# A hybrid decoder layer on one core: small products stacked into single reduced-precision passes, GLA q and k in two-product form, and the order of 512- and 256-column matmuls

## The chip, the cores and the metric

The kernel runs on one core of a Trainium2 chip. The metric is the time of one execution on the device, in microseconds (us), lower is better. Four compute engines work side by side, each with its own instruction queue: TensorE (PE, with its weight loads shown apart as PEld), VectorE (DVE), ScalarE (ACT) and GpSimd (POOL). SyncE (SP) issues most DMA transfers.

## The reference

One layer over 256 tokens of width 1024, in float32:

```
n    = RMSNorm(x)
proj = n @ W_in        # moba q,k,v (512 each) | gla q,k (512 each), v (1024) | gate-down (16)
                       # | out-gate (1024) | two branch gates (1024 each)
A = causal softmax attention over one block of 256, 8 heads of 64, RMS-normed q,k, bias by T5 bucket
log_a = log_sigmoid(gate_down @ gate_up + bias) / 16
G = gated linear attention, 4 heads (dk 128, dv 256), chunks of 64, decay exp(cumsum(log_a)),
    RMS-normed, times silu(out-gate)
x = x + (sigmoid(gA) * (A @ W_bA) + sigmoid(gG) * (G @ W_bG)) @ W_out
x = x + relu(RMSNorm(x) @ W_up)^2 @ W_down
```

## The kernel before

Every float32 operand of a large product is split into a high part (type fp32r, one pass on TensorE) and a low part, the difference. A product is then high x high + high x low + low x high. ScalarE makes the high part of a weight unit (line 94, `wH`), VectorE subtracts to get the low part (line 98, `wL`).

**Units.** The weights come in 68 units of 1 MB (`hu` counts them; `load(i)` is the DMA on SyncE, `split(i, a)` the split of half a unit). A unit is split two units ahead of its use, and load i + 4 is issued once unit i is split. The first product (MQ, units 0 and 1) takes its operands from eight transfers `xw` that hold a k-tile of x transposed and of the weights each (`first_split`, `first_block`); ahead of it TensorE runs `NWARM` warm-up matmuls.

**Order.** A loop runs over 13 column groups of 512 (`IN_ORDER`: MQ, MK, GQ, GK, MV, ...), two units each, two blocks a unit. After each block come, in program order: `flush()` (what earlier steps deferred, VectorE's subtractions above all), `split(hu + 2, ...)`, the evacuation of a finished accumulator, and the small steps that a hand-written table puts in this slot: `at(slot, step)` with slot = 2 * hu + t. Then come the branch products, W_out, and the feed-forward in eight chunks: four blocks of W_up (`block_t`), then W_down of the chunk before (`down`).

**Blocks.** `block` (lines 114 to 120) is 12 matmuls of 512 columns with tokens as the output rows. GQ and GK are made transposed, with channels as the output rows, by `block_w` (lines 131 to 138): three matmuls of 256 columns for each k, 24 a block, 192 in all. The feed-forward's `block_t` (lines 122 to 129) has high and low part of the activation side by side in one operand `a` of 512 columns, so one matmul of 512 gives high x high in the left half of the bank and high x low in the right, and one of 256 adds low x high; `ff_evac` adds the halves (lines 865, 866). There are 256 such pairs.

**Small steps that the change touches.** `make_bias` (line 274): a one-hot matrix of 33 rows times the bias table, in float32; its result goes through DRAM (`spread_bias`, `load_bias`) to the softmax. `g_diag`, `g_row` (line 478): the row of 1/rms of the tokens, `rrow`, by a float32 product with ones. `low_split`, `g_low` (lines 487, 488): the 16 gate columns, both parts stacked twice in 64 weight columns, times xH and xL. `g_decay` (lines 506, 507): for each of four heads a product of 64 rows and one of 32 rows. `g_evac` (line 544): GQ and GK times `rrow`, one VectorE operation for two heads. `g_scores` (lines 578 to 581): for each of 2 token tiles and 4 heads, three float32 products of 64 columns; a float32 matmul is two instructions. `m_transpose` (line 328) and `m_ptrans` (line 407) are float32 transposes by TensorE, four to a step.

Of the kernel before, what the change touches and what calls it, by code (L numbers as in the profile page):

```python
# [19 lines left out]
S = 256  # L20
D = 1024
NT = 2
# [7 lines left out]
NWARM = 7  # L30
# [16 lines left out]
def block_kernel(ctx, tc, xw0_d, xw_d, x_d, vec_d, wlow_d, w_d, up_d, t5_d, onehot_d, out_d):  # L47
# [6 lines left out]
    t4 = ctx.enter_context(tc.tile_pool(name="t4", bufs=22))  # L54
# [67 lines left out]
    def block_t(i, j, g, a, acc):  # L122


        for k in range(4):
# [5 lines left out]
    def block_w(i, j, g, aH, aL, acc):  # L131

        for k in range(4):
            h, c = divmod(4 * g + k, 2)
            c = slice(c * 256 + j * P, c * 256 + (j + 1) * P)
            nc.tensor.matmul(acc, wH[i][:, h, c], aH[:, k, :], start=g == 0 and k == 0, stop=False)  # L136
            nc.tensor.matmul(acc, wH[i][:, h, c], aL[:, k, :], start=False, stop=False)  # L137
            nc.tensor.matmul(acc, wL[i][:, h, c], aH[:, k, :], start=False, stop=g == 1 and k == 3)  # L138
# [5 lines left out]
    vec = const.tile([P, NVEC], F32, name="vec")  # L144
    nc.gpsimd.dma_start(vec, vec_d)
    XW = S + 512
# [11 lines left out]
    wlow = const.tile([P, 8, 16], F32, name="wlow")  # L158
    onehot = mid("onehot")[:NB + 1, :384]
    t5 = const.tile([NB + 1, H], F32, name="t5")  # L160
    nc.vector.memset(t5[NB:NB + 1, :], 1.0)
    gup = mid("gup")
    ones = const.tile([P, P], F32, name="ones")
    nc.vector.memset(ones, 1.0)
    touch = const.tile([P, 1], F32, name="touch")
    nc.scalar.activation(touch, ones[:, 0:1], AF.Exp)
# [21 lines left out]
    xH = [kview(big(f"xH{g}", F32R)) for g in range(2)]  # L188
    xL = [kview(big(f"xL{g}", F32R)) for g in range(2)]
# [61 lines left out]

    T = {}
    lowS = const.tile([P, 8, 64], F32R, name="lowS")

    def low_split():
        v = lowS.rearrange("p k (r a c) -> p k r a c", r=2, a=2)
        for r in range(2):
            nc.scalar.activation(v[:, :, r, 0, :], wlow, AF.Copy)
            nc.vector.tensor_tensor(v[:, :, r, 1, :], wlow, v[:, :, r, 0, :].bitcast(F32), op=OP.subtract)
        nc.vector.tensor_copy(causal, cf)  # L260

    def gup_split():
        both = big("gupHL", F32R)
        T["gupH"], T["gupL"] = gupH, gupL = both[:64, :512], both[:32, 512:]
        nc.scalar.activation(gupH, gup[:64, :], AF.Copy)
        nc.vector.tensor_tensor(gupL, gup[:32, :], gupH[:32, :].bitcast(F32), op=OP.subtract)
# [3 lines left out]
    bias = t4.tile([P, H, 256], F32, name="bias", tag="t8", bufs=2)  # L270
# [197 lines left out]
    def g_diag():  # L468
        T["diag"] = mid("diag")
        for t in range(NT):  # L470
            nc.vector.tensor_scalar(T["diag"][:, t * P:(t + 1) * P], ident, rstd[:, t:t + 1], None, op0=OP.mult)
# [3 lines left out]
    def g_row():  # L475

        pr = axbank("prow")
        nc.tensor.matmul(pr[:, :S], ones, T["diag"][:, :S], start=True, stop=True)
        nc.scalar.activation(rrow, pr[:, :S], AF.Copy)

    def g_low():

        p = axbank("plow")
        o = p[:64, :S]
# [4 lines left out]
        low = mid("low")[:64, :S]  # L489
        nc.vector.tensor_tensor(low, o, rrow[:64, :], op=OP.mult)  # L490

        both = t2.tile([P, 512], F32R, name="lowHL", tag="t2")
        T["lowT"], high = both[:64, :S], both[:64, S:]
        nc.scalar.activation(T["lowT"][:32], low[:32], AF.Copy)
        nc.scalar.activation(high[32:], low[32:], AF.Copy)
        nc.vector.tensor_tensor(T["lowT"][32:], low[32:], high[32:].bitcast(F32), op=OP.subtract)

    def g_decay(half):
# [3 lines left out]
        for j in range(2):  # L502
            h = 2 * half + j
            hs = slice(h * DK, (h + 1) * DK)
            o = p[:, j * S:(j + 1) * S]
            nc.tensor.matmul(o, T["gupH"][:, hs], T["lowT"], start=True, stop=False)
            nc.tensor.matmul(o, T["gupL"][:, hs], T["lowT"][:32], start=False, stop=True)
# [31 lines left out]
    def g_evac(which, half, acc):  # L539

        if half == 0:
            T[which] = big(which)
        v = T[which][:, half * 512:half * 512 + 512].rearrange("p (h t) -> p h t", h=2)
# [29 lines left out]

# [441 lines left out]
```

## Time and profile before

| | |
|---|---|
| median of 3 runs | 422.23 us (421.67 to 422.37) |
| profiled execution, its own time | 421.65 us |
| its span, first to last instruction | 419.8 us |
| busy: PE, DVE, ACT | 415.1, 281.8, 220.3 us |

The profile is of one execution. "Busy" of PE counts pipelined matmuls whose ends are modelled, so a matmul's price is better read from the start of one to the start of the next. A row of the timeline gives start, duration, engine, line, output and operands; in brackets the idle time before it and what ended it. The chain of waits is followed back from the last instruction, each piece with its start and length.

### The profile page before, as it was taken

How to read it: one execution, taken by the hardware profiler on the slowest of the kernel's cores; microseconds unless marked ns; L12 is line 12 of the kernel's file. 1: busy time of each engine (PE TensorE's matmuls, PEld its weight loads, DVE VectorE, ACT ScalarE, POOL GpSimd, SP SyncE). 2: the span in 40 equal slices, each digit the busy share in tenths (PEclk: the TensorE clock that was granted, in tenths of full speed). 3: DMA queues.
4: the chain of work that ended last, by engine and by line, in shares of the span. 5: the costliest groups of instructions: out<-in, count | busy, mean ns of one | idle time of the engine just before them, and what ended most of it. 6: DMA issues, size and time to landing. Idle time of an engine off the chain costs nothing.

```text
span 419.8 us, 5413 instructions
## 1 busy us (share of the span) xinstructions
PE 415.1 (99%) x2155; PEld 348.6 (83%) x2155; DVE 281.8 (67%) x360; ACT 220.3 (52%) x334; POOL 18.4 (4%) x22
## 2 busy tenths in 40 slices
PE   8999999999999999999999999999999999999996
PEld 5879988788888888888888888888888888888886
DVE  5739777889778653864676878757493838374753
ACT  6668456587854464552524456546453617263520
POOL 2008000000002001000000000000000000000000
PEclk9999999999999999999999999999999999999999
DMA  8895974454355343381755535736364553628002
GB/s 283 341 393 212 314 262 176 165 180 157 107 194 192 106 141 120 146 297 45 259 201 200 200 116 205 276 114 257 138 226 176 173 228 133 269 100 301 0 0 101
DMA packets 13860, 78.73 MB, mean 188 GB/s; under 512 B 1555, under 2 KB 3148, under 8 KB 5388
## 3 DMA queue, kind: packets, MB, share of 16 engines
q1 hardware_dynamic: 13372, 77.08, 50.3%
q10 hardware_dynamic: 432, 1.31, 0.9%
q8 instruction: 17, 0.28, 0.3%
q14 instruction: 7, 0.06, 0.0%
q0 software_dynamic: 32, 0.01, 0.0%
HBM read 77.33 MB, written 2.63 MB: 190 GB/s over the span
## 4 chain that ended last, share of the span: by engine, by line
PE 98%; DMA 1%; ACT 0%; DVE 0%; issue 0%
PE pu L128 14%; PE acc L118 9%; PE acc L120 9%; PE acc L119 9%; PE pu L129 7%; PE fa L118 7%; PE fa L120 7%; PE fa L119 7%; PE acc L136 2%; PE acc L137 2%; PE acc L138 2%; PE po L118 2%; PE po L120 2%; PE po L119 2%; PE pg L119 2%; PE pg L118 2%
## 5 line engine op out<-in xcount | busy, mean ns | idle before, releaser
L98 DVE TENSOR_TENSOR wl<-raw,wh 128x1024 fp32r<-128x1024 f32 x132 | 158.2, 1220 | 19.5 <-ACT wh L94 19.1
L94 ACT ACTIVATE wh<-raw 128x1024 fp32r<-128x1024 f32 x132 | 135.4, 1052 | 24.3 <-PE pg L120 9.8
L128 PE MATMUL pu<-hHL,wh 128*128 128x512 f32 x256 | 90.9, 399 | 0.0
L129 PE MATMUL pu<-hHL,wl 128*128 128x256 f32 x256 | 71.9, 281 | 0.0
L118 PE MATMUL acc<-wh,xH 128*128 128x512 f32 x160 | 64.1, 401 | 0.0
L119 PE MATMUL acc<-wl,xH 128*128 128x512 f32 x160 | 62.4, 390 | 0.0
L120 PE MATMUL acc<-wh,xL 128*128 128x512 f32 x160 | 62.4, 390 | 0.0
L128 PEld LDWEIGHTS pu<-hHL,wh 128*128 128x128 f32 x256 | 48.1, 188 | 11.8
L129 PEld LDWEIGHTS pu<-hHL,wl 128*128 128x128 f32 x256 | 48.3, 189 | 0.3
L118 PE MATMUL fa<-wh,fH 128*128 128x512 f32 x124 | 48.5, 391 | 0.0
L120 PE MATMUL fa<-wh,fL 128*128 128x512 f32 x124 | 48.4, 390 | 0.0
L119 PE MATMUL fa<-wl,fH 128*128 128x512 f32 x124 | 48.3, 389 | 0.0
L865 ACT ACTIVATE half<-pu 128x256 f32<-128x256 f32 x32 | 12.0, 378 | 55.3 <-PE pu L129 55.3
L866 DVE TENSOR_TENSOR sq<-pu,half 128x256 f32<-128x256 f32 x32 | 13.4, 422 | 35.7 <-ACT half L865 35.5
L120 PEld LDWEIGHTS acc<-wh,xL 128*128 128x128 f32 x160 | 30.0, 188 | 6.6
L118 PEld LDWEIGHTS acc<-wh,xH 128*128 128x128 f32 x160 | 30.1, 188 | 6.0
L119 PEld LDWEIGHTS acc<-wl,xH 128*128 128x128 f32 x160 | 30.1, 188 | 5.5
L120 PEld LDWEIGHTS fa<-wh,fL 128*128 128x128 f32 x124 | 23.3, 188 | 5.1
L118 PEld LDWEIGHTS fa<-wh,fH 128*128 128x128 f32 x124 | 23.3, 188 | 4.9
L119 PEld LDWEIGHTS fa<-wl,fH 128*128 128x128 f32 x124 | 23.3, 188 | 4.7
L871 ACT ACTIVATE fH<-sq 128x512 fp32r<-128x512 f32 x16 | 10.1, 634 | 20.3 <-DVE sq L868 20.3
L136 PE MATMUL acc<-xH,wh 128*128 128x256 f32 x64 | 18.6, 291 | 0.0
(234 smaller groups left out, 572.4 us busy)
## 6 DMA issues: line engine op xcount, KB each, us to landing
raw<-w SPq DMA_DIRECT2D x65, 1024.0 KB, 4.9
xw<-xw SPq DMA_DIRECT2D x7, 384.0 KB, 6.5
ur<-ud SPq DMA_DIRECT2D x1, 1536.0 KB, 10.7
raw<-w SPq DMA_DIRECT2D x2, 512.0 KB, 6.3
xs<-xs SPq DMA_DIRECT2D x2, 512.0 KB, 8.6
bias<-ur SPq DMA_DIRECT2D x1, 1024.0 KB, 7.5
xr<-xs ACTq DMA_DIRECT2D x2, 512.0 KB, 4.6
out<-o SPq DMA_DIRECT2D x3, 256.0 KB, 2.1
```

Source lines behind the costliest of these rows:

```text
L94: nc.scalar.activation(wH[i][:, s, :], raw[i][:, s, :], AF.Copy)
L98: nc.vector.tensor_tensor(wL[i][:, s, :], raw[i][:, s, :], wH[i][:, s, :].bitcast(F32), op=OP.subtract)
L118: nc.tensor.matmul(acc, aH[:, k, tk], h, start=start and k == 0, stop=False)
L119: nc.tensor.matmul(acc, aH[:, k, tk], low, start=False, stop=False)
L120: nc.tensor.matmul(acc, aL[:, k, tk], h, start=False, stop=stop and k == 3)
L128: nc.tensor.matmul(acc, wH[i][:, h, c], a[:, k, :], start=g == 0 and k == 0, stop=False)
L129: nc.tensor.matmul(acc[:, S:], wL[i][:, h, c], a[:, k, :S], start=False, stop=g == 1 and k == 3)
L136: nc.tensor.matmul(acc, wH[i][:, h, c], aH[:, k, :], start=g == 0 and k == 0, stop=False)
L137: nc.tensor.matmul(acc, wH[i][:, h, c], aL[:, k, :], start=False, stop=False)
L865: nc.scalar.activation(half, acc[:, S:], AF.Copy)
L866: nc.vector.tensor_tensor(o, acc[:, :S], half, op=OP.add)
L871: nc.scalar.activation(H, v, AF.Copy)
```

## The change

- `NWARM` goes from 7 to 9.
- Eight small transfers become three. The 16 gate columns (`wlow`) come with the constants `vec` on GpSimd's queue; bias table and one-hot matrix come in one transfer of 97 rows (two copies, 31 rows of zeros between them), the gate-up matrix in one of 96 rows (six copies). Both are split into high and low part for one fp32r product each: `make_bias` (97 rows, 384 columns), `g_decay` (96 rows, 256 columns, one matmul a head).
- `g_row` uses fp32r, with the diagonal split in two.
- GQ and GK use `block_t`; xH and xL stand side by side in one tile. Their evacuation, `g_evac`, now adds the halves of each head.
- `block_t` issues its four 512s first, then its four 256s, which add to the left half.
- `g_scores` has one float32 product of 128 columns a head, and one of 64 columns and 64 rows that overwrites a corner of it, after all four.
- Small steps move to other slots: `make_bias` 7 to 8, `g_decay(0)` 13 to 12, four of the transposes one slot later. `t4` has 20 buffers instead of 22, `t8` three instead of two.

```diff
-NWARM = 7
+NWARM = 9
@@ block_t
         for k in range(4):
-            h, c = divmod(4 * g + k, 2)
-            c = slice(c * 256 + j * P, c * 256 + (j + 1) * P)
-            nc.tensor.matmul(acc, wH[i][:, h, c], a[:, k, :], start=g == 0 and k == 0, stop=False)
-            nc.tensor.matmul(acc[:, S:], wL[i][:, h, c], a[:, k, :S], start=False, stop=g == 1 and k == 3)
+            nc.tensor.matmul(acc, tile_(wH, k), a[:, k, :], start=g == 0 and k == 0, stop=False)
         for k in range(4):
+            nc.tensor.matmul(acc[:, :S], tile_(wL, k), a[:, k, :S], start=False, stop=g == 1 and k == 3)
@@ transfers
-    nc.sync.dma_start(onehot, onehot_d)
-    nc.sync.dma_start(t5[:NB, :], t5_d)
-    nc.sync.dma_start(wlow, wlow_d)
-    for r in range(4):
-        nc.sync.dma_start(gup[16 * r:16 * r + 16, :], up_d)
+    nc.sync.dma_start(biasR, bias_d)
+    nc.sync.dma_start(gup, up_d)
     load(4)
     load(5)
@@ splits of the small operands
+        for r in range(3):
             nc.scalar.activation(v[:, :, r, 0, :], wlow, AF.Copy)
             nc.vector.tensor_tensor(v[:, :, r, 1, :], wlow, v[:, :, r, 0, :].bitcast(F32), op=OP.subtract)
...
+        nc.scalar.activation(gupS, gup, AF.Copy)
+        nc.vector.tensor_tensor(gupS[64:], gup[64:], gupS[64:].bitcast(F32), op=OP.subtract)
+    def split_bias():
+        nc.scalar.activation(biasS, biasR, AF.Copy)
+        nc.vector.tensor_tensor(biasS[64:, :H], biasR[64:, :H], biasS[64:, :H].bitcast(F32), op=OP.subtract)
@@ make_bias
-        nc.tensor.matmul(pb[:H, :384], t5, onehot, start=True, stop=True)
+        nc.tensor.matmul(pb[:H, :384], biasS[:, :H], biasS[:, H:], start=True, stop=True)
@@ g_diag, g_row
+        nc.scalar.activation(d[:, :S], full, AF.Copy)
+        nc.vector.tensor_tensor(d[:, S:], full, d[:, :S].bitcast(F32), op=OP.subtract)
...
-        nc.tensor.matmul(pr[:, :S], ones, T["diag"][:, :S], start=True, stop=True)
+        for a in range(2):
+            nc.tensor.matmul(pr[:, :S], ones, T["diag"][:, a * S:(a + 1) * S], start=a == 0, stop=a == 1)
@@ g_low
-        nc.scalar.activation(T["lowT"][:32], low[:32], AF.Copy)
-        nc.scalar.activation(high[32:], low[32:], AF.Copy)
-        nc.vector.tensor_tensor(T["lowT"][32:], low[32:], high[32:].bitcast(F32), op=OP.subtract)
+        nc.scalar.activation(both, low, AF.Copy)
+        nc.vector.tensor_tensor(both[32:64], low[32:64], both[32:64].bitcast(F32), op=OP.subtract)
@@ g_decay
-            nc.tensor.matmul(o, T["gupH"][:, hs], T["lowT"], start=True, stop=False)
-            nc.tensor.matmul(o, T["gupL"][:, hs], T["lowT"][:32], start=False, stop=True)
+            nc.tensor.matmul(p[:, j * S:(j + 1) * S], gupS[:, h * DK:(h + 1) * DK], T["low"],
+                             start=True, stop=True)
@@ g_evac
-        nc.vector.scalar_tensor_tensor(v, acc.rearrange("p (h t) -> p h t", h=2),
-                                       DK ** -0.5 if which == "gq" else 1.0,
-                                       rrow[:, None, :].to_broadcast([P, 2, S]), op0=OP.mult, op1=OP.mult)
+        half = mid("half")[:, :S]
+        nc.scalar.activation(half, acc[:, S:], AF.Copy)
+
+        def finish():
+            nc.vector.tensor_tensor(v, acc[:, :S], half, op=OP.add)
+            nc.vector.scalar_tensor_tensor(v, v, DK ** -0.5 if which == "gq" else 1.0, rrow,
+                                           op0=OP.mult, op1=OP.mult)
+
+        defer(finish)
@@ g_scores
-            nc.tensor.matmul(p[:, o:o + CH], ki[:, b:b + P], q[:, b:b + CH], start=True, stop=True)
+            nc.tensor.matmul(p[:, o:o + P], ki[:, b:b + P], q[:, b:b + P], start=True, stop=True)
+        for h in range(GH):
+            b, o = h * S + t * P, h * P
             nc.tensor.matmul(p[:CH, o + CH:o + P], kd[:, b:b + CH], q[:, b + CH:b + P],
                              start=True, stop=True)
-            nc.tensor.matmul(p[CH:, o + CH:o + P], ki[:, b + CH:b + P], q[:, b + CH:b + P],
-                             start=True, stop=True)
@@ slots
-    at(7, make_bias)
+    at(5, split_bias)
+    at(8, make_bias)
...
-    at(12, m_transpose, "mq", 0)
     at(12, m_norm, "mk", 1)
+    at(12, g_decay, 0)
+    at(13, m_transpose, "mq", 0)
     at(13, m_transpose, "mq", 1)
-    at(13, g_decay, 0)
     at(14, g_decay, 1)
-    at(14, m_transpose, "mk", 0)
     at(14, load_bias)
+    at(15, m_transpose, "mk", 0)
     at(15, m_transpose, "mk", 1)
...
-    at(28, m_ptrans, 0)
     at(29, g_exp, "edec")
+    at(29, m_ptrans, 0)
     at(29, m_ptrans, 1)
-    at(30, m_ptrans, 2)
+    at(31, m_ptrans, 2)
     at(31, m_ptrans, 3)
     at(31, g_qk, "eb")
-    at(32, m_ptrans, 4)
+    at(33, m_ptrans, 4)
     at(33, m_ptrans, 5)
@@ main loop, GQ and GK
                 if col in TRANSPOSED:
+                    acc = mmbank("acct")
                     for k in range(2):
-                        block_w(hu, t, k, xH[k], xL[k], acc[g][:, t * S:(t + 1) * S])
+                        block_t(hu, t, k, xHL[k], acc)
...
                 elif col in TRANSPOSED:
-                    if t == 1:
-                        evac[col](g, acc[g])
+                    evac[col](2 * g + t, acc)
```

## Rows read from the trace of the kernel before

**Rows 1.** The page's chain of waits, share of the span by engine.

```profile
PE 98%; DMA 1%; ACT 0%; DVE 0%; issue 0%
```

**Rows 2.** Timeline of TensorE, from the start to the second product.

```profile
0.85 3.15 PE L172 MATMUL pwarm<-const-bfloat16-1.0 128*128 128x512 bf16 x7 [0.85 <-PEq L1007]
...
4.64 0.80 PE L213 MATMUL acc<-wh,xH 128*128 128x512 f32 x1 [0.64 <-ACT wh L202]
...
8.21 0.40 PE L213 MATMUL acc<-wh,xH 128*128 128x512 f32 x1
...
17.34 0.39 PE L118 MATMUL acc<-wh,xH 128*128 128x512 f32 x1
```

**Rows 3.** Chain of waits in order of time: start, length, what.

```profile
28.38 0.74 PE pbias L274 x2
29.12 0.32 PE acc L136
...
32.19 0.43 PE prow L478 x2
...
45.95 0.44 PE pt L328 x4
...
49.69 0.31 PE pz L506
...
50.93 0.32 PE acc L136
...
55.23 0.59 PE pt L328 x4
```

**Rows 4.** Chain of waits, in the feed-forward.

```profile
272.86 0.24 PE pu L128
...
276.04 0.24 PE pu L128
```

**Rows 5.** Timeline of TensorE, a run of 256s and the 512s behind it.

```profile
149.61 0.28 PE L616 MATMUL po<-gvH,atH 128*128 128x256 f32 x1
...
150.08 0.28 PE L616 MATMUL po<-gvL,atH 128*128 128x256 f32 x1
...
151.04 0.40 PE L118 MATMUL acc<-wh,xH 128*128 128x512 f32 x1
...
151.97 0.39 PE L119 MATMUL acc<-wl,xH 128*128 128x512 f32 x1
```

**Rows 6.** Windows: length, busy PE, PEld, DVE, ACT, POOL; clock, DMA share, GB/s.

```profile
24.90:29.13 4.23, 4.23 (x19) 2.73 (x17) 1.40 (x3) 4.09 (x6) 0.70 (x1) 1.00 1.00 420
29.13:44.36 15.23, 15.23 (x127) 15.18 (x128) 14.96 (x26) 11.58 (x18) 9.15 (x5) 1.00 0.67 247
```

**Rows 7.** Timeline of VectorE, the low-rank product.

```profile
44.36 0.41 DVE L490 TENSOR_TENSOR low<-plow,rrow 64x256 f32<-64x256 f32 x1
...
45.74 0.41 DVE L496 TENSOR_TENSOR lowHL<-low,lowHL 32x256 fp32r<-32x256 f32 x1 [0.97 <-ACT lowHL L495]
```

**Rows 8.** Chain of waits, GLA scores of the first token tile.

```profile
132.89 0.17 PE pa L578 x2
133.06 0.20 PE pa L579
...
135.22 0.43 PE acc L118
```

**Rows 9.** Waits of SyncE's queue: total, times, longest (us).

```profile
SPq L85 <- DMA xs<-xs: 1.4, 1, 1.4
```

**Rows 10.** The page's DMA issues: count, KB each, median us to landing.

```profile
raw<-w SPq DMA_DIRECT2D x65, 1024.0 KB, 4.9
```

**Rows 11.** Timeline of ScalarE, the first split of load 4.

```profile
25.00 1.06 ACT L94 ACTIVATE wh<-raw 128x1024 fp32r<-128x1024 f32 x1 [5.77 <-DMA raw<-w]
```

**Rows 12.** Groups of VectorE by shape: busy us, mean ns, idle before.

```profile
L866 DVE TENSOR_TENSOR sq<-pu,half 128x256 f32<-128x256 f32 x32 | 13.4, 422 | 35.7 <-ACT half L865 35.5
...
L544 DVE SCALAR_TENSOR_TENSOR gq<-acc,rrow 128x512 f32<-128x512 f32 x2 | 1.4, 678 | 0.0
```

More of the change, by code (lines that the diff above doesn't have):

```diff
@@ L157, in block_kernel @@
     load(3)
[L158 to L164, printed above, removed]
+    NBR = 64 + NB + 1
+    smallR, smallS = big("smallR"), big("smallS", F32R)
+    biasR, biasS = smallR[:NBR, :H + 384], smallS[:NBR, :H + 384]
+    gup, gupS = smallR[:96, 512:], smallS[:96, 512:]
+    ones = const.tile([P, P], F32R, name="ones")
+    nc.vector.memset(ones.bitcast(F32), 1.0)
     touch = const.tile([P, 1], F32, name="touch")
-    nc.scalar.activation(touch, ones[:, 0:1], AF.Exp)
+    nc.scalar.activation(touch, ones[:, 0:1].bitcast(F32), AF.Exp)
     pw = axbank("pwarm")
@@ L185, in block_kernel @@
     nc.gpsimd.memset(seg.rearrange("p (c s) -> p c s", s=CH)[:, :, 0:1], 0.0)
-    xH = [kview(big(f"xH{g}", F32R)) for g in range(2)]
-    xL = [kview(big(f"xL{g}", F32R)) for g in range(2)]
+    xHL = [t4.tile([P, 4, 2 * S], F32R, name=f"xHL{g}", tag="t8", bufs=3) for g in range(2)]
+    xH, xL = [v[:, :, :S] for v in xHL], [v[:, :, S:] for v in xHL]
     for i in range(2):
@@ L252, in block_kernel @@
     T = {}
-    lowS = const.tile([P, 8, 64], F32R, name="lowS")
+    lowS = const.tile([P, 8, 96], F32R, name="lowS")
     def low_split():
-        v = lowS.rearrange("p k (r a c) -> p k r a c", r=2, a=2)
-        for r in range(2):
+        v = lowS.rearrange("p k (r a c) -> p k r a c", r=3, a=2)
+        for r in range(3):
             nc.scalar.activation(v[:, :, r, 0, :], wlow, AF.Copy)
@@ L468, in g_diag @@
     def g_diag():
-        T["diag"] = mid("diag")
+        T["diag"] = d = t2.tile([P, 512], F32R, name="diag", tag="t2")
+        full = mid("diagf")[:, :S]
         for t in range(NT):
-            nc.vector.tensor_scalar(T["diag"][:, t * P:(t + 1) * P], ident, rstd[:, t:t + 1], None, op0=OP.mult)
+            nc.vector.tensor_scalar(full[:, t * P:(t + 1) * P], ident, rstd[:, t:t + 1], None, op0=OP.mult)
+        nc.scalar.activation(d[:, :S], full, AF.Copy)
+        nc.vector.tensor_tensor(d[:, S:], full, d[:, :S].bitcast(F32), op=OP.subtract)
     rrow = const.tile([P, S], F32, name="rrow")
@@ L744, in block_kernel @@
     for u, col in enumerate(IN_ORDER):
-        acc = [(axbank if u == 1 else mmbank)(f"acc{t}") for t in range(NT)]
+        acc = [] if col in TRANSPOSED else [(axbank if u == 1 else mmbank)(f"acc{t}") for t in range(NT)]
         for g in range(2):
@@ L809, in block_kernel @@
     hres = [big(f"h{t}") for t in range(NT)]
-    hHL = [t4.tile([P, 4, 2 * S], F32R, name=f"hHL{g}", tag="t8", bufs=2) for g in range(2)]
+    hHL = [t4.tile([P, 4, 2 * S], F32R, name=f"hHL{g}", tag="t8", bufs=3) for g in range(2)]
     hss = [small(f"hss{t}", 2) for t in range(NT)]
@@ L992 @@
     cols = lambda v, n: A(v)[0].reshape(n, 128).T
+    bias = np.concatenate([np.concatenate([A(t5_bias), np.ones((1, 8), np.float32)]), _onehot()], axis=1)
     arrays = {
@@ L998 @@
             cols(norm2_g, 8), cols(gla_gate_bias, 4), cols(gla_out_norm_g, 2),
[L999 to L1000 removed]
+            np.tile(A(moba_q_norm_g)[0], 2)[:, None], np.tile(A(moba_k_norm_g)[0], 2)[:, None],
+            w[:, GLOW:GLOW + 16].reshape(8, 128, 16).transpose(1, 0, 2).reshape(128, 128)], axis=1),
         "w": np.stack(units),
[L1002 to L1004 removed]
+        "gup": np.tile(A(gla_gate_up)[0], (6, 1)),
+        "bias": np.concatenate([bias, np.zeros((31, 8 + 384), np.float32), bias]),
     }
```

44 lines of the change are left out of this document (15 added, 29 removed).

## The prediction, made before the change was built or run

> **What bounds the kernel now.** I read the chain of waits first: 98% of it is TensorE [rows 1], so time goes down only where TensorE's own work shrinks, and only as long as no other engine becomes what TensorE waits for. Then I read the stretches that the change touches. At the start, seven warm-ups run from 0.85 us, TensorE then idles for 0.64 us, the first product starts at 4.64 us at about 0.43 us a matmul (1.2 GHz) and falls to 0.23 us (2.4 GHz) at 8.21 us [rows 2]; from there 40 matmuls of 512 columns take 9.13 us, 0.228 us each. Around the GLA columns, the chain in order of time shows small products as pieces that are dear for their size [rows 3]. In the feed-forward, 512s and 256s alternate: 9 pairs in 3.18 us, 0.353 us a pair [rows 4]; elsewhere twelve 256s stand in a row, and 512s follow them [rows 5]. The reader should see next that VectorE is full just there: busy for 14.96 of the 15.23 us before it evacuates the low-rank product [rows 6]. TensorE doesn't wait for it today, because the product that needs the result stands some 3.4 us behind it (the split ends at 45.74 + 0.41 = 46.15 us [rows 7], the product starts at 49.69 us in the chain [rows 3]). The change moves that product one block earlier.
>
> **The change part by part.**
>
> *Bias product.* Two passes of float32 take 0.74 us, and the next matmul takes 0.32 us in place of 0.12 us: 0.94 us [rows 3]. One pass of 384 columns over 97 rows takes by columns about 0.17 us (384/512 of 0.228 us [rows 2]). Saved: 0.77 us; 0.57 us if the 0.2 us of the change of shape stays.
>
> *Row of rstd.* 0.43 us [rows 3] becomes two 256s at 0.12 us [rows 5]: 0.19 us saved.
>
> *Decay product.* Today each half is four matmuls at 0.31 us, and the matmul behind it is 0.20 us (first half) or 0.15 us (second) late: 1.44 + 1.39 = 2.83 us [rows 3]. After it each half is two matmuls of 256 columns and 96 rows. No row has 96. The bounds are 0.12 us (128 rows [rows 5]) and 0.31 us (64 and 32 rows in turn). In the latter each matmul differs in shape from the one before, which the four new ones don't, so I take 0.12: 0.48 us, 2.35 us saved; with 0.31 us and the 0.35 us of late followers 1.24 us. The Trainium skill, "TensorEngine Tiling (Array Packing)", section Tiling Modes, knows row tiles of 128, 64 and 32 and a drain between modes, so 96 rows would count as 128; no row shows it, and by it the sum is the one taken.
>
> *GLA q and k.* 192 matmuls at 0.12 us are 23.04 us. After it there are 16 groups of four 512s and four 256s. Four 512s right behind 256s took 0.93 us (151.04 to 151.97), four 256s behind a 512 took 0.47 us (149.61 to 150.08) [rows 5]: 1.40 us a group, 22.45 us, 0.6 us saved. Bounds: with no price for the alternation 4 x 0.228 + 4 x 0.12 = 1.39 us (0.8 saved), with the alternating price 1.41 us (0.4 saved).
>
> *Feed-forward order.* 64 such groups: 1.413 us now (four pairs of 0.353 us), 1.40 us after, some 11 ns each, 0.7 us; 0 to 1.6 us by the same bounds. One rule speaks against it. The Trainium skill, "TensorE: Matmul & The Clock Gate", section LDWEIGHTS, prices a weight load by its columns, 128 in 107 ns, as much as 256 columns stream in; by it the order would be neutral and the sum 0.7 us smaller. The rows give 0.12 us to a 256 in a run and 0.353 us to a pair, so the measured difference stays in.
>
> *Scores.* In the chain, from 132.89 to the next block at 135.22 us, plus 0.20 us by which that block's first matmul is long (0.43 us against 0.23): 2.53 us, twice [rows 8]. The first one with 64 weight columns takes 0.20 us in the chain [rows 8] where half of the 0.11 us of a float32 instruction of 128 columns (0.44 us for four transposes [rows 3]) would be its share, so a change of shape costs some 0.15 us, four times each way. After: eight at 0.11, one change in, eight of the small ones at most 0.11 each, one change out with the 0.20: 0.88 + 0.15 + 0.88 + 0.20 = 2.11 us. Saved 0.4 us each, 0.8 us; with small ones at half and no changes 1.32 us, 2.4 us saved; at the other end 0.
>
> *Warm-ups.* Two more at 0.43 us fill the 0.64 us idle and end about when the first operands do; delay up to 0.2 us. If the clock rises by 4.64 us instead of at 8.21 us, at most half of these 3.57 us comes back, 1.8 us; at least nothing. I cost it at nothing, since the wait below swallows it.
>
> *Transfers.* SyncE issues load 4 (the first GLA weights) only when an x transfer has landed [rows 9], behind seven small transfers, so the queue is empty before it. Such loads take 4.9 us from issue to landing [rows 10], 2.5 us of it data at 420 GB/s [rows 6]; some 2.4 us are start-up that a load in a busy queue doesn't show. After the change two small transfers remain and load 4 can queue up behind x. Against that, the small ones carry some 100 KB more (about 340 KB instead of 243 KB by their shapes), and the gate weights' 64 KB go ahead with the constants on GpSimd's queue, 0.4 us together at 420 GB/s. ScalarE starts on load 4 at 25.00 us today, after 5.77 us of waiting [rows 11]; I take 1.8 us earlier, 23.2 us, of at most 2.4 us and at least none.
>
> *VectorE's queue, and what is late next.* The stretch of 15.23 us starts 4.1 us behind ScalarE's first split of load 4 (29.13 against 25.00 us), so 1.8 us earlier; ScalarE's new split of the bias operands (392 elements, about 0.45 us) stands ahead of it: 27.8 us. Into the stretch come the diagonal's split (a wait for ScalarE and a subtraction, 0.85 us), a third copy of the gate weights (0.2 us), and the GLA evacuation: three heads at two operations of about 0.4 us net of overlap (0.42 us for 256 elements) in place of two at 0.6 us (0.68 us) [rows 12], 1.0 us. So the low product is evacuated at 27.8 + 15.23 + 2.05 = 45.1 us. From there to the split operand it is 1.79 us today (44.36 to 46.15 us [rows 7]), less one of two ScalarE copies: ready at 46.45 us. TensorE gets to the decay product, now behind the block that ends at 45.95 us [rows 3], at 45.95 - 0.77 - 0.19 - 0.37 (ten of the 16 groups) = 44.6 us. So it waits for 46.45 - 44.6 = **1.9 us of new idle time**. Behind this wait stand all GK blocks but the first, so the whole rest of the kernel moves with it.
>
> *At nothing:* the moved transposes (0.44 us for four wherever they stand [rows 3]); their splits are used a block or two later, and if that cover goes a split costs 0.6 us of VectorE. The bias product one block later: its round trip through DRAM waits for its turn on SyncE's queue anyway; if not, the softmax starts late, blocks ahead of its use. The low product keeps its 16 matmuls of 256 columns. Buffer counts: four long-lived tiles leave the pool that loses two.
>
> **Sum.** Up to the GLA v columns: -(0.77 + 0.19 + 2.35 + 0.6) + 1.9 = -2.0 us. Scores -0.8, feed-forward -0.7: **-3.5 us**. Against the profiled execution's own 421.65 us (span 419.8 us, 1.85 us around it) that is 418.15 us; the median lies 0.58 us higher, so I predict **418.7 us**. What a measurement of this kernel can tell from no change is about 0.2%, 0.84 us.
>
> **Rivals.**
> 1. *No new wait* (0.13). VectorE gets through sooner, and all that TensorE saves counts, with up to 1.1 us of the clock's: -5.4 to -6.5 us, some 416.3 us. For: load 4 might land even earlier. Against: VectorE's 98% in that stretch.
> 2. *Load 4 is no earlier* (0.10): the new wait is 3.7 us, the sum -1.7 us, 420.5 us. For: small rows still stand ahead. Against: the wait on x that goes away.
> 3. *The small prices don't fall* (0.12): 96 rows cost 0.31 us (-1.1 of the gain) and the feed-forward's order is worth nothing, a weight load being hidden as well behind either neighbour (-0.7): -1.7 us, 420.5 us.
> 4. *Slower* (0.05): the two transfers of 96 and 97 rows ahead of load 4 hold it up. Each microsecond past 23.2 us is one of waiting before the decay product; at 26.7 us the gain is gone, at 27.5 us it is measurably slower. Against: at 420 GB/s they are 0.85 us.
> 5. *No change to be seen* (0.05): several of these halves; and some of 2 and 3 ends there.
>
> The forecast has 0.55, with 417.6 to 419.9 us of its own. The range takes in the bounds and cases 1 to 3 in part: 416.2 to 420.9 us. Faster by over 0.2% (under 421.4 us): 0.85; within: 0.10; slower: 0.05.
>
> **What would show it.** The decay product in two pieces of 0.24 us with about 1.9 us idle ahead of the first one, ended by VectorE's split of the low product; load 4's split starting near 23 us; groups of 1.40 us in the feed-forward, 0.23 us for a 512 and 0.12 us for a 256; scores at 2.1 us a tile. It is wrong if TensorE waits elsewhere, or if that wait is gone.

## The result, and the profile after

The changed kernel takes 428.24 us (426.75 to 428.62), the kernel before 422.3 us in the same runs: ratio 1.0133, 95% interval 1.0102 to 1.0164. It is 1.3% slower, where 418.7 us was forecast. The profiled execution took 427.91 us, its span 426.2 us, 6.4 us more than before.

The page's chain of waits, share of the span by engine, answers to [rows 1]:

```profile
PE 86%; DMA 4%; DVE 3%; ACT 3%; SPq 2%; issue 1%; ACTq 0%
```

TensorE had 98% of it; now 14% of what sets the end lies elsewhere, in DMA first. Where the new waits stand shows in the timeline of TensorE (start, duration, then in brackets the idle time before it and what ended it):

```profile
4.56 0.64 PE L209 MATMUL acc<-wh,xHL 128*128 128x512 f32 x1
5.04 0.40 PE L210 MATMUL acc<-wh,xHL 128*128 128x512 f32 x1
...
8.69 0.50 PE L209 MATMUL acc<-wh,xHL 128*128 128x512 f32 x1 [0.82 <-ACT wh L198]
...
27.68 0.39 PE L120 MATMUL acc<-wh,xHL 128*128 128x512 f32 x1
31.96 1.91 PE L131 MATMUL acct<-xHL,wh 128*128 128x512 f32 x4 [3.90 <-ACT wh L94]
33.68 1.05 PE L133 MATMUL acct<-xHL,wl 128*128 128x256 f32 x4
34.99 1.46 PE L131 MATMUL acct<-xHL,wh 128*128 128x512 f32 x4 [0.26 <-ACT wh L94]
36.85 0.74 PE L133 MATMUL acct<-xHL,wl 128*128 128x256 f32 x4 [0.40 <-DVE wl L98]
37.43 0.34 PE L270 MATMUL pbias<-smallS 97*8 97x384 f32 x1
38.48 0.84 PE L478 MATMUL prow<-diag,ones 128*128 128x256 f32 x2 [0.72 <-ACT diag L469]
...
55.02 0.50 PE L503 MATMUL pz<-lowHL,smallS 96*128 96x256 f32 x2 [2.59 <-DVE lowHL L495]
```

The reader is to see five waits, 7.87 us together: 3.90 us at the first GLA block, for ScalarE's split of load 4; 0.26 and 0.40 us at the pieces behind it; 0.72 us at the row of 1/rms; and 2.59 us at the decay product, which is the new wait of the forecast (1.9 us). The start is as forecast or better: 0.23 us a matmul from 5.04 us on, where [rows 2] has it from 8.21 us; the 0.82 us of waiting for weights at 8.69 us takes most of that back, and the second product starts at 17.02 us, 0.32 us earlier.

The windows give the clock (length, busy PE, PEld, DVE, ACT, POOL, then granted clock, DMA share, GB/s):

```profile
20.70:28.40 7.70, 7.36 (x33) 5.77 (x31) 0.36 (x1) 0.00 (x0) 0.00 (x0) 1.00 1.02 344
28.40:30.75 2.35, 0.00 (x0) 0.00 (x0) 0.00 (x0) 0.00 (x0) 0.00 (x0) 1.00 1.00 415
...
32.17:35.58 3.41, 3.15 (x9) 2.37 (x9) 1.35 (x4) 3.41 (x7) 0.72 (x1) 0.50 0.07 29
...
56.06:59.48 3.42, 3.42 (x13) 2.93 (x12) 2.84 (x7) 1.45 (x3) 0.00 (x0) 0.50 0.99 307
```

Behind the 3.90 us and behind the 2.59 us the clock is granted at 0.50, the level of 1.2 GHz. The 3.15 and 3.42 us of matmuls in these two stretches would have taken half the time at the full clock: 3.3 us more of TensorE's own work. What the kernel lost by it is less sure. Within the first stretch TensorE waits for splits even at the lower clock, and from load 4's landing to the decay product the chain of waits runs through ScalarE and VectorE, not through TensorE. Three of its pieces (start, length):

```profile
33.99 0.95 ACT wh L94
...
35.57 1.23 DVE wl L98
...
54.55 0.42 DVE lowHL L495
```

Why load 4 is late: SyncE's timeline (start, duration of the issue) and the chain's first piece behind 17 us.

```profile
11.71 0.32 SPq L226 DMA_DIRECT2D smallR<-bias  x1
12.07 5.61 SPq L227 DMA_DIRECT2D smallR<-gup  x1
17.79 19.41 SPq L85 DMA_DIRECT2D raw<-w  x5
```

```profile
17.79 12.96 DMA raw<-w
```

Load 4 is issued at 17.79 us, 2.4 us earlier than before (its issue stood at 20.16 us), and lands 12.96 us later, at 30.75 us. ScalarE's first split of it answers to [rows 11]:

```profile
30.86 1.06 ACT L94 ACTIVATE wh<-raw 128x1024 fp32r<-128x1024 f32 x1 [11.24 <-DMA raw<-w]
```

30.86 us, in place of 25.00 us before and the 23.2 us of the forecast. The trace's packets say what lay in between. The bias transfer is 97 packets of 1568 bytes; here they are counted from the packet records, beside two kernels that come in the experiments:

```
kernel                     rows  first and last start   step between starts   8 KB packets per us, 20 to 27 us
changed                      97   18.83 to 27.03 us       85 ns                 37.1
pad106                      106   18.26 to 23.64 us       51 ns                 38.3
pad112                      112   18.24 to 19.64 us       13 ns                 48.6
```

With 97 rows the packets start one by one over 8.2 us (the expectations below say 19.5 to 27.1 us; the records give 18.83 to 27.03). From 32 to 37 us, when this kernel's loads should be far ahead, only 3.4 packets of 8 KB start in a microsecond, about what one DMA engine does at 0.31 us a packet. The records name no engine, but this fits one of the 16 that is late with its share of every load, while a load has landed only when the last share has. Loads 4 to 7 land 2.47 us apart, at 30.75, 33.23, 35.71 and 38.18 us, eight such packets each.

Farther back the terms of the forecast are there. The first GLA score tile, and groups in the feed-forward, as in [rows 8] and [rows 4]:

```profile
141.37 1.05 PE L582 MATMUL pa<-eb,einv 128*128 128x128 f32 x8
142.35 0.68 PE L585 MATMUL pa<-eb,edec 128*64 128x64 f32 x8
142.96 0.50 PE L118 MATMUL acc<-wh,xHL 128*128 128x512 f32 x1
...
278.88 1.07 PE L131 MATMUL pu<-hHL,wh 128*128 128x512 f32 x4
279.79 0.64 PE L133 MATMUL pu<-hHL,wl 128*128 128x256 f32 x4
280.26 1.09 PE L131 MATMUL pu<-hHL,wh 128*128 128x512 f32 x4
```

A tile takes 1.59 us to the next block's start (before 2.41 us), a group 280.26 - 278.88 = 1.38 us here, and 1.41 us among the GLA blocks. From the first to the last matmul of W_up, with W_down's in between, it is 155.94 us, before 156.73 us.

One table for all that follows: the first matmul of some steps, in us before, and how many us later or earlier it starts in each profiled execution.

| first matmul of | before | changed | pad112 | pad106 | pad112_decay13 | pool_mult | best |
|---|---|---|---|---|---|---|---|
| row of 1/rms | 32.03 | +6.45 | -0.75 | +3.11 | +0.32 | +0.26 | -0.37 |
| decay product | 49.62 | +5.40 | -1.80 | +2.04 | +0.07 | +0.05 | -0.75 |
| MoBA scores, first | 61.80 | +8.35 | -0.42 | +4.78 | -1.11 | -1.94 | -3.04 |
| MoBA scores, second | 71.69 | +8.72 | +1.24 | +5.18 | +0.39 | -1.41 | -2.68 |
| GLA scores | 132.73 | +8.64 | +1.06 | +5.00 | +0.21 | -1.58 | -2.85 |
| feed-forward | 237.62 | +7.04 | -0.55 | +3.40 | -1.40 | -3.19 | -4.45 |
| the last of all | 416.32 | +6.23 | -1.35 | +2.60 | -2.20 | -3.99 | -5.26 |

The changed kernel loses 8.4 us ahead of the MoBA scores and gets 2.4 us of them back behind.

### The profile page after: what moved, and what is told of

Same layout as the page of the kernel before. It is cut to its first block, busy times and chain, and to the rows that moved or that the text cites. A ratio compares the mean times of both kernels' runs of the same rounds, so it can differ in the third digit from the quotient of the medians.

```text
span 426.2 us, 5265 instructions
## 1 busy us (share of the span) xinstructions
PE 413.2 (97%) x2072; PEld 345.0 (81%) x2072; DVE 286.1 (67%) x374; ACT 223.0 (52%) x344; POOL 18.6 (4%) x22
## 4 chain that ended last, share of the span: by engine, by line
PE 86%; DMA 4%; DVE 3%; ACT 3%; SPq 2%; issue 1%; ACTq 0%
PE pu L131 14%; PE acc L118 8%; PE acc L119 8%; PE acc L120 8%; PE pu L133 7%; PE fa L119 7%; PE fa L120 7%; PE fa L118 7%; DMA raw<-w 3%; PE po L120 2%; PE po L118 2%; PE pg L118 2%; PE po L119 2%; PE pg L120 2%; PE pg L119 2%; PE acct L131 2%
## 5 line engine op out<-in xcount | busy, mean ns | idle before, releaser
L131 PE MATMUL pu<-hHL,wh 128*128 128x512 f32 x256 | 69.9, 394 | 0.0
L118 PE MATMUL acc<-wh,xHL 128*128 128x512 f32 x160 | 63.9, 399 | 0.0
L120 PE MATMUL acc<-wh,xHL 128*128 128x512 f32 x160 | 62.5, 390 | 0.0
L119 PE MATMUL acc<-wl,xHL 128*128 128x512 f32 x160 | 62.4, 390 | 0.0
L131 PEld LDWEIGHTS pu<-hHL,wh 128*128 128x128 f32 x256 | 44.2, 189 | 6.3
L133 PEld LDWEIGHTS pu<-hHL,wl 128*128 128x128 f32 x256 | 39.3, 189 | 5.4
L133 PE MATMUL pu<-hHL,wl 128*128 128x256 f32 x256 | 40.7, 281 | 0.0
L120 PEld LDWEIGHTS acc<-wh,xHL 128*128 128x128 f32 x160 | 30.0, 188 | 6.6
L118 PEld LDWEIGHTS acc<-wh,xHL 128*128 128x128 f32 x160 | 30.1, 188 | 6.2
L119 PEld LDWEIGHTS acc<-wl,xHL 128*128 128x128 f32 x160 | 30.1, 188 | 5.6
L131 PE MATMUL acct<-xHL,wh 128*128 128x512 f32 x64 | 19.7, 434 | 4.2 <-ACT wh L94 4.2
```

The costliest lines, as they stand in the source:

```text
L118: nc.tensor.matmul(acc, aH[:, k, tk], h, start=start and k == 0, stop=False)
L119: nc.tensor.matmul(acc, aH[:, k, tk], low, start=False, stop=False)
L120: nc.tensor.matmul(acc, aL[:, k, tk], h, start=False, stop=stop and k == 3)
L131: nc.tensor.matmul(acc, tile_(wH, k), a[:, k, :], start=g == 0 and k == 0, stop=False)
L133: nc.tensor.matmul(acc[:, :S], tile_(wL, k), a[:, k, :S], start=False, stop=g == 1 and k == 3)
```

## Experiments

**The transfer of 97 rows, padded (pad112, pad106).** Nothing but the number of rows in one transfer differs from the changed kernel.

```diff
-    nc.sync.dma_start(biasR, bias_d)
+    nc.sync.dma_start(smallR[:112, :H + 384], bias_d)      # and 15 rows of zeros in bias_d; pad106: 106, 9 rows
```

> The changed kernel with fifteen rows of zeros added to the bias transfer: 112 rows (171.5 KB) in place of 97, nothing else. Theory A (the 97 rows go through a single DMA engine: in the trace of the changed kernel its 97 packets of 1568 bytes start one behind the other, about 12 in a microsecond from 19.5 to 27.1 us, and the loads behind it each wait for that engine): the packets now move side by side, load 4 lands by about 24 us in place of 30.75, TensorE's 4.3 us of idle time ahead of GQ and the fall of the clock behind it are gone; of the 8.3 us lost up to the MV column at least 5.5 come back, time 419 to 422.5 us. The Trainium skill, page DMA: Bandwidth & Descriptors, section Why a DMA increments its semaphore by 16 and not by 1, says that a transfer uses the largest number of engines up to 16 that divides its rows: 16 for 112 and one for 97, which speaks for A. Theory B (many small rows ahead of load 4 are dear whatever their number): more rows, no earlier, 428 to 429 us. Theory C (VectorE and ScalarE have too much to do around the GLA columns, the transfers are innocent): load 4 earlier, the time within 1 us of 428.2.

> The same with 106 rows (2 x 53). Theory A: two engines, so 53 packets each at 83 ns, 4.4 us in place of 8.1; load 4 lands some 3.7 us before 30.75, at about 27 us, so TensorE's idle time ahead of GQ shrinks from 4.3 us to 0.5 to 1 us; time between those with 112 and with 97 rows, 421 to 425 us. By the rule of the Trainium skill (page DMA: Bandwidth & Descriptors, section Why a DMA increments its semaphore by 16 and not by 1) 106 rows go through two engines. Theory B: as with 97 rows, 428 us or a little more, and the same with 112.

Measured: 112 rows 421.58 us (ratio to before 0.9978, 0.9959 to 0.9998), 106 rows 424.22 us (1.0033, 1.0017 to 1.0048), against 428.24 us with 97. ScalarE's first split of load 4 with 112 rows, and the window in which the changed kernel moved 344 GB/s:

```profile
23.65 1.06 ACT L94 ACTIVATE wh<-raw 128x1024 fp32r<-128x1024 f32 x1 [4.63 <-DMA raw<-w]
```

```profile
20.70:28.40 7.70, 7.70 (x37) 6.42 (x36) 1.59 (x4) 4.75 (x8) 0.72 (x1) 1.00 1.02 418
```

Theory A holds, and B is out: 15 more rows save 6.7 us. C as it was put is out too. Load 4 lands at 23.54 us with 112 rows, at 27.40 us with 106 (27 was expected) and at 30.75 us with 97. The issue of the gate-up transfer behind it takes SyncE 0.43, 2.05 and 5.61 us. In the profiled execution with 112 rows, the fastest of its twelve, the clock is granted in full throughout; in ten of the twelve its mean is 0.991 to 0.996, so there the clock fell for a stretch. The Trainium skill, "DMA: Bandwidth & Descriptors", section Why a DMA increments its semaphore by 16 and not by 1, says that a transfer is spread over the largest number of engines up to 16 that divides its rows, which makes 1, 2 and 16 of 97, 106 and 112; the steps of 85, 51 and 13 ns agree in order, if not in exact proportion.

But something of C is left: the kernel with 112 rows gains 0.8 us where 3.5 was forecast. Its waits of TensorE between 20 and 100 us (engine and line, waited for, us, times, longest), and the timelines at the largest of them:

```profile
PE pz L503 <- DVE lowHL L495: 2.6, 1, 2.6
PE ps L334 <- DVE mkL L288: 1.3, 1, 1.3
PE prow L478 <- ACT diag L469: 0.7, 1, 0.7
```

```profile
44.59 0.63 PE L133 MATMUL acct<-xHL,wl 128*128 128x256 f32 x4
47.82 0.50 PE L503 MATMUL pz<-lowHL,smallS 96*128 96x256 f32 x2 [2.60 <-DVE lowHL L495]
```

```profile
43.87 1.22 DVE L98 TENSOR_TENSOR wl<-raw,wh 128x1024 fp32r<-128x1024 f32 x1
45.00 0.42 DVE L545 TENSOR_TENSOR gq<-acct,half 128x256 f32<-128x256 f32 x1
45.45 0.42 DVE L546 SCALAR_TENSOR_TENSOR gq<-gq,rrow 128x256 f32<-128x256 f32 x1
45.80 0.68 DVE L316 TENSOR_TENSOR mk<-mk,rsm 128x512 f32<-128x512 f32 x1
46.40 0.41 DVE L491 TENSOR_TENSOR low<-plow,rrow 96x256 f32<-96x256 f32 x1
47.35 0.41 DVE L495 TENSOR_TENSOR lowHL<-low,lowHL 32x256 fp32r<-32x256 f32 x1 [0.54 <-ACT lowHL L494]
```

VectorE comes to the low product at 46.40 us straight from other work, and TensorE had been through its block since 45.2 us.

**The same cost added to the kernel before (before_97).**

```diff
+    extra = const.tile([97, 392], F32, name="extra")
+    nc.sync.dma_start(extra, xw_d[0, :97, :392])
     load(4)
```

> The kernel before with one transfer added and nothing else: 97 rows of 392 numbers of the first weights into a tile that nobody reads, issued on SyncE's queue just ahead of load 4. Theory A: load 4 lands about 6 to 8 us later than its 24.90 us, TensorE idles some 3 to 5 us ahead of GQ, its clock falls; 426 to 431 us. Theory B: 0.4 to 1 us. Theory C: no difference beyond 0.5 us.

Measured: 429.61 us (1.0154, 1.0126 to 1.0182), 7.2 us slower, by one transfer of 149 KB that nobody reads. TensorE's largest wait is the one of the changed kernel:

```profile
PE acc L136 <- ACT wh L94: 4.6, 1, 4.6
```

Load 4 lands at about 32.7 us. Theory A again, without any other part of the change, so the work of VectorE and ScalarE is out as the cause of the slowdown.

**The same 97 rows on another queue (act_97).**

```diff
-    nc.sync.dma_start(biasR, bias_d)
+    nc.scalar.dma_start(biasR, bias_d)
```

> The changed kernel with its transfer of 97 rows left whole, but issued on ScalarE's queue in place of SyncE's, at the same place of the program; all else as in the changed kernel. It asks whether load 4 is late because it stands behind the 97 packets in the same queue (theory A1) or because the one engine's time is lost to it whatever the queue (A2). A1: the engine takes packets of both queues in turn, load 4's eight of 8 KB are each at most one small packet late (8 x 0.08 = 0.7 us), load 4 lands at 24 to 26 us, time 421 to 423.5 us. A2: the engine owes the same 8 us before it is through, load 4 lands near 30 us, time 426 to 428.5 us.

Measured: 429.86 us (1.018, 1.0144 to 1.0216). The time lies above both ranges, but load 4 lands at 25.85 us, as A1 had it, so it was the place behind the 97 packets in the queue that held it up. But now the 97 packets wait their turn among those of the loads, mostly 2 to 5 a microsecond, and start from 16.17 to 36.82 us. ScalarE's split of them stands in its queue ahead of all later weight splits:

```profile
29.00 1.04 ACT L94 ACTIVATE wh<-raw 128x1024 fp32r<-128x1024 f32 x1
37.37 0.53 ACT L265 ACTIVATE smallS<-smallR 97x392 fp32r<-97x392 f32 x1 [7.33 <-DMA smallR<-bias]
```

VectorE's subtraction of it stands ahead of the weights' low parts in the same way, and TensorE waits for what is behind:

```profile
PE acct L133 <- DVE wl L98: 8.1, 1, 8.1
```

From 34.76 to 45.00 us, during and behind this wait, the clock is granted at 0.50. My figure for A1 left out that somebody waits for the transfer itself.

**The decay product at its old place (pad112_decay13).**

```diff
+    at(12, m_transpose, "mq", 0)
     at(12, m_norm, "mk", 1)
-    at(12, g_decay, 0)
-    at(13, m_transpose, "mq", 0)
     at(13, m_transpose, "mq", 1)
+    at(13, g_decay, 0)
```

(and the first `mk` transpose back from slot 15 to 14). These two transposes are all that goes back: of the transposes the change moves five, not four, and the three `m_ptrans` stay where it put them.

> The changed kernel with 112 rows, and the decay product of the first half behind the transposes of slot 13 again, as in the kernel before (the four moved transposes go back too). My step of the new wait (the product one block earlier waits for VectorE's split of the low product, 1.9 us forecast, 2.8 us measured in the changed kernel): no wait ahead of the decay product; 1 to 3.5 us less than with 112 rows alone (the larger figure if the wait there also lets the clock fall). Rival: with load 4 back early VectorE is through in time, no wait is left with 112 rows alone, and the two are within 0.5 us.

Measured: 419.83 us (0.9936, 0.9911 to 0.9961), 1.75 us less than with 112 rows alone, in the range expected, and the wait of 2.6 us is gone (2.59 us in the changed kernel too, not the 2.8 us of the expectation). Part of the 1.75 us is the clock: its mean is at 0.995 or 0.996 in three executions of seven here, in ten of twelve with 112 rows alone. Among those at the full clock (0.999 or more), four of 418.94 to 419.83 us against two of 420.32 and 420.71 us, the gain is about 1.1 us. Less came back than 2.6 us, for others stand in the view of waits:

```profile
PE ps L334 <- DVE mkL L288: 1.1, 1, 1.1
PE pt L324 <- DVE mqL L288: 0.9, 1, 0.9
```

Both are VectorE's again, one and two blocks farther on.

**VectorE relieved, in two ways (gla_three, pool_mult).** Both start from pad112_decay13. The first puts GQ and GK back into three products with the old evacuation; the second keeps two products:

```diff
-        nc.scalar.activation(half, acc[:, S:], AF.Copy)
+        scale = DK ** -0.5 if which == "gq" else 1.0
+        nc.scalar.activation(half, acc[:, S:], AF.Copy, scale=scale)
...
-            nc.vector.tensor_tensor(v, acc[:, :S], half, op=OP.add)
-            nc.vector.scalar_tensor_tensor(v, v, DK ** -0.5 if which == "gq" else 1.0, rrow,
-                                           op0=OP.mult, op1=OP.mult)
+            nc.vector.scalar_tensor_tensor(v, acc[:, :S], scale, half, op0=OP.mult, op1=OP.add)
+            nc.gpsimd.tensor_tensor(v, v, rrow, op=OP.mult)
```

> The version with 112 rows and the decay product at its old place, and in it GQ and GK in three products of 256 columns again, with the old evacuation (one VectorE operation for two heads). Theory D (the two-product form costs more than it saves: in the trace of the version with 112 rows its evacuation puts eight pairs of VectorE operations, some 0.79 us a pair, in place of four of 0.6 us into a stretch in which VectorE is full; TensorE pays for these 3.9 us in waits ahead of the MoBA transposes, 0.93 us, and of the MoBA scores, 1.13 us): the waits go, 0.6 us of TensorE's comes back as work, so some 1.4 us faster, 418.2 to 419 us. Rival (the waits are set by the DMA of the loads or by the order of the small steps): 0.6 us slower, 420.4 us, and the waits stay.

> The same version (112 rows, old place of the decay product), with GQ and GK in the two-product form, but the multiplication by the row of 1/rms done by GpSimd from SBUF, and the scale folded into the sum of the halves: one VectorE operation a head in place of two, some 3.4 us less for VectorE. Theory D: both waits of TensorE (0.93 and 1.13 us) go, and the 0.6 us of the two-product form stay: 417.6 to 418.6 us. Rival: GpSimd's operation holds VectorE up, or the waits come from elsewhere: 419.8 us, unchanged.

Measured: 418.58 us (0.9903, 0.9868 to 0.9938) and 417.71 us (0.9883, 0.9856 to 0.9911). Both stand where theory D put them: the waits at the transposes are gone from both traces, that at the MoBA scores from the first, and 0.2 us of it is left in the second. So with its evacuation on VectorE the two-product form likely cost more in waits than it saved on TensorE, by 1.25 us of the medians; the intervals of 419.83 and 418.58 us overlap, so the times alone do not show it. The multiplication on GpSimd, with the scale folded in, is worth 2.1 us of the medians; the two intervals touch at 0.9911. That pool_mult is better than gla_three is likely, not shown: their intervals overlap, and in the profiled execution of gla_three TensorE waited 2.0 us for the splits of the first GLA weights. Whether the edit has a part in that is not shown: three products need the first low part after two matmuls, the two-product form after four. A TensorE that comes 2.0 us later also leaves VectorE that time, so pool_mult is the cleaner test of what the later waits come from.

**The decay product early, with VectorE relieved (pool_decay12).** pad112 with the second of these edits.

> The changed kernel with 112 rows and with the multiplication of GQ and GK by the row of 1/rms on GpSimd; the decay product stands one block earlier, as in the changed kernel. If the wait ahead of it (2.60 us with 112 rows alone) is VectorE's backlog of weight splits and evacuations: three heads' second operation of 0.43 us are gone ahead of the low product, the wait falls to some 1.3 us, the waits behind it (1.29 us ahead of the MoBA scores) go; 418 to 419 us. Rival (the wait is the chain from the last matmul of the low product through VectorE, ScalarE and VectorE, 1.4 us, and does not depend on what else VectorE has): it stays at 2.6 us, 420.5 to 421.5 us.

Measured: 420.84 us, from 418.22 to 423.07 (0.9951, 0.9926 to 0.9976). The time is the rival's. All ten executions are longer than the longest of pool_mult (417.95 us), which differs by the places of the decay product and of two transposes alone, and the intervals are apart: the earlier place costs about 3 us with VectorE relieved too. How it costs them is only in part shown, since the profiled execution is one of the longest at 422.89 us and ScalarE's split of load 4 began at 26.77 us in it, 3.1 us later than in pad112. A split on VectorE, the wait, and the window behind it:

```profile
46.47 1.76 DVE L98 TENSOR_TENSOR wl<-raw,wh 128x1024 fp32r<-128x1024 f32 x1
```

```profile
50.51 0.79 PE L503 MATMUL pz<-lowHL,smallS 96*128 96x256 f32 x2 [2.17 <-DVE lowHL L495]
```

```profile
50.50:53.91 3.41, 3.40 (x11) 3.02 (x12) 2.87 (x5) 2.03 (x5) 1.11 (x1) 0.50 1.06 357
```

The wait is neither the 1.3 us of my theory nor the rival's 2.6: VectorE is still busy when TensorE is through at 48.34 us, and it comes to the low product at 49.09 us. A weight split there took 1.76 us in place of 1.22 beside GpSimd's multiplication, which takes back part of what that saved. Behind the wait the clock is at 0.50; in eight of the ten executions its mean is 0.994 to 0.996, and the two others, 418.22 and 419.03 us, are the shortest.

**Seven warm-ups (warm7).** pad112_decay13 with `NWARM = 7`.

> The same version (112 rows, old place of the decay product) with seven warm-ups in place of nine. In the trace with nine the clock is at 2.4 GHz from about 4 to 5 us, in that of the kernel before from 8.2 us, and the second product starts 0.6 to 1 us earlier. My step (the warm-ups count for nothing, because the wait on VectorE behind swallows what they give): within 0.5 us of 419.8. Rival (the head is bound by TensorE once the transfer is mended): 0.5 to 1 us slower.

Measured: 419.21 us (0.9934, 0.9906 to 0.9961), against 419.83 us with nine, with intervals that overlap widely: no difference that can be told, and if any, seven are not slower. It lies 0.6 us under the 419.8, just outside the 0.5 us of my step. The reason was not the one I gave: the clock rose early with seven as well (last section), and MQ's own weight splits then hold TensorE up, for 0.50 us at 8.30 us here and 0.70 us at 8.46 us with nine.

**The two late parts alone (before_tail).** The kernel before with the new `block_t` in the feed-forward and the new `g_scores`.

> The kernel before with two parts of the change alone, both far behind the GLA columns: the order of the feed-forward's matmuls (four 512s, then four 256s) and the scores with one product of 128 columns a head. By the traces of both kernels: feed-forward 0.8 us shorter (156.73 to 155.94 us from its first to its last matmul), a score tile 0.8 us shorter each, so 2.4 us faster, 419.8 to 420.2 us. Rival (a matmul's weights load as well behind either neighbour, so the order is neutral, which is what the Trainium skill's page TensorE: Matmul & The Clock Gate, section LDWEIGHTS, would make of it; only the scores gain): 420.7 us.

Measured: 420.05 us (0.995, 0.9931 to 0.9969). The feed-forward takes 155.94 us and a score tile 1.59 us in this trace too, 0.79 and twice 0.82 us less than before. The time alone would not exclude the rival (0.9969 is 420.75 us); the trace does. One thing goes with the order that no run separates from it: the 256s now add to the left half of the bank, not to the right.

**A better version (best).** pool_mult with load 4 ahead of the small transfers, and the diagonal made by VectorE alone:

```diff
+    load(4)
     nc.sync.dma_start(smallR[:112, :H + 384], bias_d)
     nc.sync.dma_start(gup, up_d)
-    load(4)
@@ g_diag
-            nc.vector.tensor_scalar(full[:, t * P:(t + 1) * P], ident, rstd[:, t:t + 1], None, op0=OP.mult)
-        nc.scalar.activation(d[:, :S], full, AF.Copy)
-        nc.vector.tensor_tensor(d[:, S:], full, d[:, :S].bitcast(F32), op=OP.subtract)
+            hi, lo = (d[:, a + t * P:a + (t + 1) * P] for a in (0, S))
+            nc.vector.tensor_scalar(hi, ident, rstd[:, t:t + 1], None, op0=OP.mult)
+            nc.vector.scalar_tensor_tensor(lo, ident, rstd[:, t:t + 1], hi.bitcast(F32),
+                                           op0=OP.mult, op1=OP.subtract)
```

> The version with 112 rows, the decay product at its old place and the multiplication on GpSimd (417.71 us), and two more edits: load 4 is issued ahead of the two small transfers, and VectorE makes both parts of the diagonal of 1/rms from the identity, without the trip through ScalarE. Load 4 lands at about 23 us in place of 23.5 to 24.6; the wait ahead of the row of 1/rms (0.72 us) falls to under 0.2 us and the waits for the first weight splits (0.3 to 1.7 us in some executions) go: 416.5 to 417.4 us. Rival: the bias split, now fed later, holds ScalarE up and with it the splits behind it: 417.7 us or more.

Measured: 416.02 us (0.9844, 0.9821 to 0.9868), 1.6% faster than the kernel before and a little better than expected. All that TensorE still waits for:

```profile
PE pwarm L168 <- PEq L1012: 0.8, 1, 0.8
PE acc L209 <- ACT wh L198: 0.5, 1, 0.5
PE prow L478 <- DVE diag L468: 0.4, 1, 0.4
```

The row's wait fell to 0.4 us, not under 0.2. Load 4's split began at 24.00 us in this execution, no earlier than in pad112, so what the order of issues gave is not separated from the rest.

## Why the prediction was wrong

The step that failed is the fourth load's start: "I take 1.8 us earlier, 23.2 us, of at most 2.4 us and at least none". It priced the transfers ahead of load 4 by their bytes at 420 GB/s, which supposes that every transfer is spread over all 16 engines. One of 97 rows was not: its packets went one behind the other for 8.2 us, as through one engine, and ScalarE began on load 4 at 30.86 us. The lower bound, "at least none", excluded a loss without a reason. Rival 4 named this delay, without its cause, and gave it 0.05: by its price, a microsecond for each past 23.2 us, 7.66 us late make the time 418.7 + 7.7 = 426.4 us; the rest up to 428.24 us may be in the clock, which fell behind the idle time. The rival also had the place wrong: the new idle time stands ahead of the first GLA block (3.90 us), while the wait before the decay product stays at 2.59 us. The rival's "Against: at 420 GB/s they are 0.85 us" was the same error once more.

The other steps, by the traces:

- *New wait at the decay product*, 1.9 us forecast: 2.59 us, and 2.60 us with load 4 mended. Right in place and cause, too small in size. The low product's evacuation came at 46.40 us where 45.1 was forecast. By its own terms the GLA evacuation is 1.2 us and not 1.0 (three times 0.8 less twice 0.6). What the forecast left out is that the backlog doesn't end there: eight evacuations of two operations each fill VectorE up to MV, and the MoBA scores wait 1.29 us for it (pad112).
- *Row of 1/rms*: 0.19 us of gain forecast. The two matmuls take 0.68 us in place of 0.43, and wait 0.72 us for the diagonal's trip through ScalarE. I costed that trip only as work of VectorE.
- *Decay product*: 0.34 and 0.24 us for the two halves, where 0.24 each was forecast: 96 rows take 0.12 us. The Trainium skill's rule (TensorEngine Tiling (Array Packing), Tiling Modes) agrees with that.
- *Bias product*: one pass takes 0.34 us, not 0.17 us, so 0.6 us is saved and not 0.77. That is its own length; what stands behind it is a wait, so there is no next start to price it by.
- *GLA q and k*: the groups cost 1.38 to 1.41 us, as forecast. The gain was there, and gone in VectorE's queue.
- *Feed-forward*: 0.79 us saved, 0.7 forecast (the upper bound of 1.6 us comes to 1.4 by its own numbers). By the Trainium skill's section LDWEIGHTS (TensorE: Matmul & The Clock Gate) the order would be neutral; the measurement decides against that, with 155.94 against 156.73 us.
- *Scores*: 0.82 us saved a tile, 0.4 forecast. The eight small products take 0.61 us together, under 0.08 each, where I had 0.11 and two changes of shape.
- *Warm-ups at nothing*: no run shows otherwise (warm7), but the reason was not the wait on VectorE farther back.

In the changed kernel's profiled execution, along TensorE's own time, the waits (7.87 us) and the halved clock (3.3 us) make 11.2 us; the start, the bias and decay products and the GLA groups, less the row, give back about 3 us (0.32 + 0.6 + 2.2 + 0.3 - 0.25). That leaves 8.0 of the 8.35 us by which the MoBA scores start late; 0.3 us stays unexplained. This says where the time stands, not what each part would give back alone. With 112 rows and no other edit the median misses the forecast by 2.9 us. The profiled execution misses it by 2.2 us (420.32 against the 418.15 us for a profiled one): there the waits above, 0.7 us more than forecast at the decay product, 0.72 at the row and 1.29 us at the MoBA scores, outweigh what came out better. The median's other part is likely the clock, which none of the terms allowed for: a mean of 0.996 is an estimated 1.7 us (0.004 of 420), and ten of twelve executions have that or less.

## What to carry to other kernels

Before a transfer is priced by its bytes, ask over how many DMA engines its number of rows lets it spread: here 15 rows of zeros were worth 6.7 us, and the loads behind it paid, not the transfer's own user. An engine that is busy for 98% of a stretch takes no more operations, however short; a form that saves TensorE 0.04 us a group and costs VectorE more operations a head was likely a loss here until one of them was moved. Look at the granted clock of every run, and not at the profiled one alone: with 112 rows the profile shows the full clock, and ten of twelve runs did not have it. And where a lower bound says "at least none", look for what could make it a loss.

## What the hardware showed that was not expected

- While the 97 packets went through, the other engines were slower too: 37.1 packets of 8 KB a microsecond from 20 to 27 us against 51.5 from 28 to 30 us, a median of 0.39 us a packet in place of 0.31. The share of busy DMA time was about 1.0 in both stretches and showed nothing; GB/s did, with 344 and 415.
- Waits of 2.59, 2.62 and 2.17 us ahead of the decay product were followed by the half clock in the changed kernel, pad106 and pool_decay12; one of 2.60 us in the profiled execution of pad112 was not. By the mean clock the fall is the common case with the product at its early place (ten of twelve executions of pad112, eight of ten of pool_decay12) and less common at the old one (three of seven of pad112_decay13, one of four of pool_mult).
- The number of warm-ups did not set when the clock rose. By the spacing of the matmuls, which goes from 0.43 to 0.23 us, it rose at 8.21 us in the profile before, but by 4.98 us in that of warm7, with seven warm-ups as well; with nine it rose by 5.04 us in the changed kernel and at 6.43 us in best. The spacing has to tell it: the windows show 1.00 from 4.64 to 8.20 us for the kernel before too.
- While GpSimd multiplies, VectorE is slower: the split of half a unit takes 1.22 us alone and 1.75 us (43.11 us, in best) beside it. GpSimd's multiplication takes 0.73 to 1.12 us. Beside another operation of GpSimd, the one that makes `rsm`, the split takes 1.22 us as well (41.04 us, in best).
